# A third pair of split-weight tiles in two weight rings, a smaller scratch for dynamic DMAs, and new ranks and paces for interleaved streams

## The chip, the core and the metric

The kernel is one program on one core of a Trainium2 chip. TensorE (PE in the profile) multiplies matrices, with its weight loads shown apart as PEld; VectorE (DVE) and ScalarE (ACT) work on elements, GpSimd (POOL) fills tiles and issues the DMAs of its own queue, and SyncE (SP) issues the loads. Each engine runs its own instructions in program order, and waits where an operand or a tile is not free yet. The metric is device time in microseconds (us) of one execution; lower is better.

## What is computed

Two layers of a hybrid transformer trunk over 512 latent tokens and 256 context tokens, model width 1024, all in float32. The reference, cut to one layer:

```
mod  = silu(c) @ w_mod[l] + b_mod[l]                 # six vectors of 1024; the same for the context
h    = modulate(rmsnorm(x,   norm1_g[l]), sh1, sc1)  # 512 latent tokens
hc   = modulate(rmsnorm(ctx, norm1_g[l]), ...)       # 256 context tokens
y, yc = hybrid_mixer(h, hc, ...)   # one input projection, then side by side:
#   (A) gated DeltaNet, 8 heads, both directions: short conv, chunks of 64 with a triangular solve
#       in each, then a scan over the chunks; the latent scan starts from the context's last state
#   (B) latent attention, 8 heads: latent queries attend to context and latent keys
#   then one output projection of both
x = x + g1 * y
x = x + g2 * swiglu(modulate(rmsnorm(x, norm2_g[l]), sh2, sc2), w_gate[l], w_up[l], w_down[l])
# the context goes through the same output projection and FFN, in layer 0 only
return rmsnorm(x, final_norm_g)                      # after both layers
```

## The kernel before

**Split weights.** The large products run as three products of float32r tiles: a weight tile `w` is split into `hi` (a copy in float32r) and `lo = w - hi`, and so are the activations; `gemm` (L195) issues `hi*hi`, `hi*lo` and `lo*hi` for each block of 128 rows. `load_w` (L174) loads a weight in pieces of 512 columns: a DMA on SP into a raw tile (L183), a copy on ACT for `hi` (`cpy`, which the profile shows as L132), and a subtraction on DVE for `lo` (`tt`, shown as L120). There are two rings of these tiles: ring `w` for the latent stream (raw `wr`, halves `wh` and `wl`) and ring `f` for the context stream (`fr`, `fh`, `fl`). A ring holds two pairs `hi`/`lo`; `RAWS` (L45) gives ring `w` two raw tiles and ring `f` three. A weight of 1024 columns takes two pieces, so it fills a ring. A third way to load, ring `g`, brings a weight unsplit and is used only by the context's first input projection.

`pipelined` (L209) emits the load of weight i+1, its copies and subtractions too, just before the matmuls of weight i. A new tile of a ring waits until the last reader of the tile whose place it takes is done.

**Streams.** The program's order is made by `weave` (L59). Each part of the network is a generator, a stream, that emits some instructions and then yields either a condition to wait for or a triple: how long the piece lasts, what it costs TensorE, and what it costs VectorE, in the planner's own microseconds. `weave` keeps a time for each stream and one clock for each of the two engines, and takes next the stream with the smallest

```
    s = min(ready, key=lambda r: (max(r.t, clock[0]), r.rank, r.t))
    ...
    end = s.t + r[0]
    for i, c in enumerate(r[1:]):
        clock[i] = max(clock[i], s.t) + c
        end = max(end, clock[i])
```

so that among streams behind the TensorE clock the rank decides, the lower one first, and each piece pulls its stream up to both clocks. The streams that matter here, with their ranks before: `ctx_chain` and `lat_chain` (0; `gdn_pre`, with the triangular solve in 31 steps on DVE and transposes around it, then `gdn_scan`), `ctx_in`, `ctx_mla` and `mod_rest` (1; the modulation vectors, 16 units of 1 MB of weights each after the first 8), `lat_in` (2; normalize, then 20 input projections of one 1024-column weight each), `ctx_ffn` and `ctx_in1` (3), `mla_prep` (4; queries, keys and row maxima of four head pairs), `mla_att` (5; attention of the four pairs), `lat_ffn` (6). `mod_rest`, `lat_in`, `lat_chain`, `ctx_chain`, `mla_prep`, `mla_att` and `lat_ffn` exist once for each layer. `paced` (L1293) multiplies the triples of a stream by a factor: 0.6 for `lat_chain` and 1.5 for `mla_prep`, in layer 1 only.

In the order of time: context input projections; latent input projections with the context chain and `mod_rest` between them; `ctx_mla`; `ctx_ffn` with the first latent chain; attention of layer 0; `lat_ffn` with `ctx_in1` and the second context chain; layer 1 with `lat_in`, the latent chain and attention; at last `lat_ffn` alone.

**DMAs of POOL.** GpSimd issues the DMAs that copy rotary parts between tiles (`fill_rope`, L798), spill activations (L236, L1077) and bring the gates' rows back broadcast over partitions (L450). For the descriptors of these dynamic DMAs, a scratch is set aside in each partition of the on-chip memory.

Of the kernel before, what the change touches and what calls it, by code (L numbers as in the profile page):

```python
# [41 lines left out]
LAT = SimpleNamespace(n=NL, nch=8, off=NC_, mi=0, h="hx", t="t", w="w")  # L42
BUFS = {"hx": 16, "m": 12, "g4": 16, "hd": 7, "t": 4, "ox": 7, "kc": 4, "tc": 3, "st": 1}
WIDTH = {"hx": 512, "m": 512, "g4": 1024, "hd": 512, "t": 516, "ox": 512, "kc": 256, "tc": 260, "st": 512}
RAWS = {"w": 2, "f": 3}  # L45
PSB = {"A": 2, "M": 1, "F": 1, "B": 2, "C": 2}
CHUNK_AT = {("tail", 0): 0, ("ckv", 0): 17, ("cq", 0): 18, ("cq", 1): 19}
CHUNK_AT.update({(m, j): 1 + 4 * j + i for j in range(4) for i, m in enumerate("kqvz")})


PACE = {("lat_chain", 1): 0.6, ("mla_prep", 1): 1.5}


class Stream:
# [32 lines left out]
def trunk_kernel(ctx, tc, xin, cc, wmod, small, win, wuq, wuk, wuv, wout, wgu, wdn, cst, rope, out):  # L87
# [16 lines left out]
    def nm(s):  # L104
        uid[0] += 1
        return f"{s}_{uid[0]}"
# [67 lines left out]
    def load_w(src, n, ring):  # L174
        if ring == "g":
            big = slot("g4")
            nc.sync.dma_start(out=big[:, 0:n], in_=src)
            return big
        halves = []
        for a in range(0, n, 512):  # L180
            m = min(512, n - a)
            raw = raw_tile(ring)[:, 0:m]
            nc.sync.dma_start(out=raw, in_=src[:, a:a + m])  # L183
            hi = wp.tile([P, 512], F32R, name=nm(ring + "h"), tag=ring + "h", bufs=2)[:, 0:m]
            lo = wp.tile([P, 512], F32R, name=nm(ring + "l"), tag=ring + "l", bufs=2)[:, 0:m]
            cpy(hi, raw)
            tt(lo, raw, hi, SUB)
            halves.append((hi, lo))
        return halves
# [940 lines left out]
    def ctx_in():  # L1130
        v.xc = load_x(CTX, xin[:, :, 0:NC_])
        v.mod = [Mod(0)]
        for _ in v.mod[0].ticks(8, "g4"):
            pass
        v.xx = load_x(LAT, xin[:, :, NC_:])
        yield 35, 0, 21.0
        hc = modulated(CTX, v.xc, v.mod[0].al[:, 0], v.mod[0].t, 0, "F", True)
        v.c = [Mix(0, CTX, hc, [CALL], True, "A", "hd", "hd")]
        yield 5, 0, 3.0
        yield from v.c[0].inproj([("tail", 0)] + KQV[CALL], "g")  # L1140
        done.add("ckqv")
        yield from v.c[0].inproj(CQS + ZS, "g")
        done.add("cin")

    def ctx_chain(l):
        yield need("ckqv" if l == 0 else "c1kv")
        c = v.c[l]
        yield from c.stage(CALL)
        yield from c.scan(CALL)
        done.add(f"cscan{l}")  # L1150
        if l == 0:
            yield need("cin")
            c.gate(CALL)
            done.add("cg")

    def ctx_mla():
        yield need("cin")
        c = v.c[0]
        v.kvc = [mla_norm(0, CTX, [c.ckv], 8.0, KN, "F")[0]]
        cqc = mla_norm(0, CTX, c.cq, 4.0, QN, "F")  # L1160
        v.K = [keys(CTX, c.kr)]
        yield 6, 0, 3.6
        v.yc = []
        yield need("mod0")
        yield from mla_ctx(0, cqc, v.kvc[0], *v.K[0], v.yc)
        done.add("cmla")

    def ctx_ffn():
        yield need("cg", "cmla", "norm0")
        c, modt = v.c[0], v.mod[0].t  # L1170
        ys = ysplit(CTX, [c.o[j] for j in range(4)] + v.yc)
        v.xc = load_x(CTX, xin[:, :, 0:NC_])
        yield 5, 0, 3.0
        yield from outproj(0, CTX, ys, v.xc, modt, "FM")
        h2 = modulated(CTX, v.xc, v.mod[0].al[:, 1], modt, 24, "F")
        yield 8, 0, 4.8
        yield from ffn(0, CTX, v.xc, h2, modt, ("F", "M"))
        v.cs = dp.tile([KD, P, NC_], F32, name=nm("cscr"), tag=nm("cscr"))
        spill(v.xc, v.cs)
        done.add("cffn")  # L1180

    def ctx_in1():
        yield need("cffn", "att30")
        nmod = Mod(1)
        v.mod.append(nmod)
        yield from nmod.ticks(8, "m")
        done.add("head1")
        yield need("out0")
        v.xc = load_x(CTX, v.cs)
        hc = modulated(CTX, v.xc, nmod.al[:, 0], nmod.t, 0, "F")  # L1190
        c = Mix(1, CTX, hc, [CALL], False, "F", None, None)
        v.c.append(c)
        yield 8, 0, 4.8
        yield from c.inproj([("tail", 0)] + [(m, hj) for hj in range(4) for m in "kv"])
        done.add("c1kv")
        yield from c.inproj([("ckv", 0)])
        v.kvc.append(mla_norm(1, CTX, [c.ckv], 8.0, KN, "F")[0])
        v.K.append(keys(CTX, c.kr))
        done.add("c1")

    def mod_rest(l):
        yield need("cin" if l == 0 else "start1")
        yield from v.mod[l].ticks(16, "m")
        done.add(f"mod{l}")
# [85 lines left out]
            yield need("c1", "cscan1")  # L1290
            done.add("start1")

    def paced(gen, l):  # L1293
        f = PACE.get((gen.__name__, l), 1)
        for r in gen(l):
            yield r if callable(r) else tuple(f * a for a in r)

    streams = [(1, ctx_in()), (1, ctx_mla()), (3, ctx_ffn()), (3, ctx_in1())]
    for l in range(DEPTH):
        streams += [(0, ctx_chain(l)), (1, mod_rest(l)), (2, lat_in(l)), (0, paced(lat_chain, l)),  # L1300
                    (4, paced(mla_prep, l)), (5, mla_att(l)), (6, lat_ffn(l))]
    weave(streams)
    xx = v.xx
    pr = rms_rows(LAT, xx, 1.0, "A")
    for k in range(KD):
# [123 lines left out]
```

## Time and profile before

| | |
|---|---|
| median of 3 runs | 2268.44 us (2268.09 to 2271.84) |
| the profiled execution | 2272.16 us, of which 2270.4 us from the first to the last instruction |
| TensorE busy | 2090.8 us (92% of the span) |
| VectorE busy | 1448.1 us (64%) |
| ScalarE busy | 885.3 us (39%) |
| granted TensorE clock, mean | 0.953 of full speed |

Busy time is the time in which the profile shows an instruction of the engine at work. A busy TensorE is not TensorE at its peak: at a lower granted clock the same matmul is busy for longer.

### The profile page before, as it was taken

The numbers are of one execution on the slowest core, as the hardware profiler recorded it, in microseconds if no ns is written. First come the engines' busy times: TensorE is split into PE (matmuls) and PEld (weight loads), VectorE is DVE, ScalarE is ACT, GpSimd is POOL, SyncE is SP. The second block draws the span as 40 slices with busy tenths as digits, with TensorE's granted clock in tenths as the row PEclk, the third lists the DMA queues.
The fourth block names the chain that finished last, engine by engine and source line by source line (L and its number), as shares of the span: only waits on it lengthen the run. The fifth ranks groups of instructions, "written<-read, shape, count | busy, mean of one in ns | idle before, by whom it ended". The sixth has DMA issues, their size and how long they took to land.

```text
span 2270.4 us, 40544 instructions
## 1 busy us (share of the span) xinstructions
PE 2090.8 (92%) x16016; PEld 1616.3 (71%) x16016; DVE 1448.1 (64%) x2846; ACT 885.3 (39%) x1579; POOL 134.3 (6%) x307
## 2 busy tenths in 40 slices
PE   6989988899999999899999999996987998999996
PEld 3856677789887646678788885675654676888885
DVE  4668758976787653788544447898667355444445
ACT  3342355443435344552332234435343234222233
POOL 0200003000201000010000000200020000000000
PEclk9999998899999999999999999997997999999998
DMA  8336513343433143252222336531010012333322
GB/s 328 116 112 202 185 29 109 116 141 113 139 121 109 48 131 110 74 159 89 85 79 89 98 94 231 166 104 41 20 47 13 30 65 70 98 98 97 95 96 88
DMA packets 130639, 240.43 MB, mean 106 GB/s; under 512 B 15184, under 2 KB 30064, under 8 KB 130448
## 3 DMA queue, kind: packets, MB, share of 16 engines
q1 hardware_dynamic: 124592, 224.10, 30.4%
q0 software_dynamic: 5856, 13.74, 2.3%
q8 instruction: 126, 2.06, 0.4%
q14 instruction: 65, 0.53, 0.1%
HBM read 228.24 MB, written 6.91 MB: 104 GB/s over the span
## 4 chain that ended last, share of the span: by engine, by line
PE 74%; DVE 14%; DMA 5%; ACT 4%; issue 3%; SPq 0%; ACTq 0%; DVEq 0%; POOL 0%; POOLq 0%
PE psA L202 31%; PE psM L202 14%; PE psF L202 5%; PE psA L952 4%; PE psA L207 3%; PE psB L949 3%; PE psM L271 2%; PE psB L598 2%; DVE g L120 2%; DVE wl L120 1%; PE psC L645 1%; ACT t L132 1%; DVE g L129 1%; PE psC L668 1%; DVE fl L120 1%
## 5 line engine op out<-in xcount | busy, mean ns | idle before, releaser
L202 PE MATMUL psA<-hx,wh 128*128 128x512 f32 x1680 | 546.5, 403 | 26.8 <-ACT hx L132 17.0
L132 ACT ACTIVATE wh<-wr 128x512 fp32r<-128x512 f32 (+2 forms) x410 | 249.1, 608 | 674.6 <-PE psA L202 439.1
L120 DVE TENSOR_TENSOR wl<-wr,wh 128x512 fp32r<-128x512 f32 (+2 forms) x410 | 272.2, 665 | 244.2 <-ACT wh L132 241.8
L202 PEld LDWEIGHTS psA<-hx,wh 128*128 128x128 f32 x1680 | 316.7, 191 | 124.7 <-issue 20.7
L202 PE MATMUL psA<-hx,wl 128*128 128x512 f32 x840 | 333.9, 398 | 7.0 <-DVE wl L120 7.0
L202 PE MATMUL psM<-hx,wh 128*128 128x512 f32 x704 | 217.9, 390 | 1.5 <-ACT wh L132 1.5
L202 PEld LDWEIGHTS psA<-hx,wl 128*128 128x128 f32 x840 | 160.4, 191 | 49.4 <-DVE wl L120 10.4
L132 ACT ACTIVATE fh<-fr 128x512 fp32r<-128x512 f32 (+3 forms) x186 | 111.1, 600 | 170.5 <-PE psF L202 72.8
L129 DVE SCALAR_TENSOR_TENSOR g<-psA,mod,g 128x512 f32<-128x512 f32 x112 | 84.0, 750 | 111.4 <-PE psA L202 111.1
L120 DVE TENSOR_TENSOR fl<-fr,fh 128x512 fp32r<-128x512 f32 (+3 forms) x186 | 122.5, 660 | 48.2 <-ACT fh L132 42.6
L202 PEld LDWEIGHTS psM<-hx,wh 128*128 128x128 f32 x704 | 131.9, 188 | 29.7 <-ACT wh L132 2.8
L202 PE MATMUL psM<-hx,wl 128*128 128x512 f32 x352 | 137.4, 390 | 1.1 <-DVE wl L120 1.1
L202 PE MATMUL psF<-m,fh 128*128 128x256 f32 x600 | 115.1, 288 | 10.2 <-ACT m L132 7.4
L202 PE MATMUL psA<-hd,wh 128*128 128x512 f32 x384 | 120.6, 393 | 0.0
L952 PE MATMUL psA<-t,m 128*128 128x512 f32 x192 | 107.8, 670 | 3.9 <-ACT t L132 3.7
L202 PEld LDWEIGHTS psF<-m,fh 128*128 128x128 f32 x600 | 94.4, 192 | 17.6 <-ACT m L132 8.7
L202 PE MATMUL psA<-ox,wh 128*128 128x512 f32 x320 | 100.7, 393 | 0.0
L132 ACT ACTIVATE t<-psB 128x512 f32<-128x512 f32 x96 | 56.3, 596 | 91.4 <-PE psB L949 79.2
L202 PE MATMUL psF<-m,fl 128*128 128x256 f32 x300 | 86.8, 289 | 0.9 <-DVE fl L120 0.7
L202 PE MATMUL psM<-m,fh 128*128 128x256 f32 x416 | 83.7, 299 | 3.9 <-ACT m L132 2.1
L202 PEld LDWEIGHTS psA<-hd,wh 128*128 128x128 f32 x384 | 71.6, 188 | 16.7 <-DVE hd L120 1.1
L207 PE MATMUL psA<-m,g 128*128 128x256 f32 x320 | 74.4, 393 | 6.2 <-DMA g<-win 4.0
(378 smaller groups left out, 3710.8 us busy)
## 6 DMA issues: line engine op xcount, KB each, us to landing
wr<-wgu SPq DMA_DIRECT2D x176, 256.0 KB, 2.6
m<-wmod SPq DMA_DIRECT2D x160, 256.0 KB, 4.2
fr<-wgu SPq DMA_DIRECT2D x88, 256.0 KB, 2.7
wr<-win SPq DMA_DIRECT2D x80, 256.0 KB, 3.1
wr<-wdn SPq DMA_DIRECT2D x64, 256.0 KB, 2.6
g<-win SPq DMA_DIRECT2D x20, 512.0 KB, 6.6
g<-wmod SPq DMA_DIRECT2D x16, 512.0 KB, 10.2
fr<-wdn SPq DMA_DIRECT2D x32, 256.0 KB, 2.8
```

The source lines that it names most:

```text
L120: (e or V).tensor_tensor(out=out, in0=a, in1=b, op=op)
L129: V.scalar_tensor_tensor(out=out, in0=a, scalar=s, in1=b, op0=op0, op1=op1)
L132: A.activation(out, a, f, **kw)
L202: PE.matmul(o, ww[:, wk], xx if n is None else xx[:, a:a + n], start=cnt == 0, stop=cnt == 3 * nk - 1)
L207: PE.matmul(o, w[:, k * P:k * P + P], x_, start=k == 0, stop=k == len(xs) - 1)
L271: PE.matmul(o[32 * j:32 * j + 32, :], sc[:, k, :], parts[j], start=k == 0, stop=k == KD - 1, tile_position=(0, 32 * j))
L598: PE.matmul(pv[s, q, d, :], u3(lh[d])[s, c, :], u3(rh[d])[s, c, :], start=True, stop=True)
L645: PE.matmul(o[s], x_[s], y_[s], start=i == 0, stop=i == len(mm) - 1)
L668: PE.matmul(v4(kv)[s, hi, d, :], u3(ks[d])[s, unit(hi, n, d), :], v4(u)[s, hi, d, :], start=True, stop=True)
L949: PE.matmul(pst, K[ki][:, b:b + P], Q[qi], start=cnt == 0, stop=cnt == 2)
L952: PE.matmul(py, v.vt[i, j][:, hp:hp + 2, :].rearrange("p z e -> p (z e)"), pt, start=i == 0, stop=i == 5)
```

## The change

Both rings get a third pair of `hi`/`lo` tiles, and ring `w` a third raw tile. These are 10 KB more in each partition (five tiles of 512 float32). The scratch for dynamic DMAs is given a size, 2048 bytes. The table `TUNE` takes the place of the ranks in the code and of `PACE`: it names a rank and a pace for each stream and layer. Against before these entries differ: `ctx_mla` has rank 0 (was 1); `ctx_ffn` pace 0.93 (was 1); `lat_in` pace 2.0 in both layers (was 1); `mla_prep` pace 1.07 in layer 0 (was 1), and in layer 1 rank 2 (was 4) and pace 1.275 (was 1.5); `mod_rest` of layer 1 pace 0.7 (was 1). Everything else of the planner is as before.

```diff
-RAWS = {"w": 2, "f": 3}
+RAWS = {"w": 3, "f": 3}
...
-PACE = {("lat_chain", 1): 0.6, ("mla_prep", 1): 1.5}
+TUNE = {
+    ("ctx_in", 0): (1, 1.0),
+    ("ctx_mla", 0): (0, 1.0),
+    ("ctx_ffn", 0): (3, 0.93),
+    ("ctx_in1", 0): (3, 1.0),
+    ("ctx_chain", 0): (0, 1.0),
+    ("mod_rest", 0): (1, 1.0),
+    ("lat_in", 0): (2, 2.0),
+    ("lat_chain", 0): (0, 1.0),
+    ("mla_prep", 0): (4, 1.07),
+    ("mla_att", 0): (5, 1.0),
+    ("lat_ffn", 0): (6, 1.0),
+    ("ctx_chain", 1): (0, 1.0),
+    ("mod_rest", 1): (1, 0.7),
+    ("lat_in", 1): (2, 2.0),
+    ("lat_chain", 1): (0, 0.6),
+    ("mla_prep", 1): (2, 1.275),
+    ("mla_att", 1): (5, 1.0),
+    ("lat_ffn", 1): (6, 1.0),
+}
...
-            hi = wp.tile([P, 512], F32R, name=nm(ring + "h"), tag=ring + "h", bufs=2)[:, 0:m]
-            lo = wp.tile([P, 512], F32R, name=nm(ring + "l"), tag=ring + "l", bufs=2)[:, 0:m]
+            hi = wp.tile([P, 512], F32R, name=nm(ring + "h"), tag=ring + "h", bufs=3)[:, 0:m]
+            lo = wp.tile([P, 512], F32R, name=nm(ring + "l"), tag=ring + "l", bufs=3)[:, 0:m]
...
-    streams = [(1, ctx_in()), (1, ctx_mla()), (3, ctx_ffn()), (3, ctx_in1())]
-    for l in range(DEPTH):
-        streams += [(0, ctx_chain(l)), (1, mod_rest(l)), (2, lat_in(l)), (0, paced(lat_chain, l)),
-                    (4, paced(mla_prep, l)), (5, mla_att(l)), (6, lat_ffn(l))]
-    weave(streams)
+    once = (ctx_in, ctx_mla, ctx_ffn, ctx_in1)
+    per_layer = (ctx_chain, mod_rest, lat_in, lat_chain, mla_prep, mla_att, lat_ffn)
+    todo = [(g, 0, ()) for g in once] + [(g, l, (l,)) for l in range(DEPTH) for g in per_layer]
+    weave([(TUNE[g.__name__, l][0], paced(g(*a), TUNE[g.__name__, l][1])) for g, l, a in todo])
...
-    nc = bacc.Bacc("TRN2", target_bir_lowering=False, num_devices=1)
+    nc = bacc.Bacc("TRN2", target_bir_lowering=False, num_devices=1, dynamic_dma_scratch_size=2048)
```

## Rows read from the trace of the kernel before

**Rows 1.** The page: busy time, granted clock in 40 slices, chain that ended last.

```profile
PE 2090.8 (92%) x16016; PEld 1616.3 (71%) x16016; DVE 1448.1 (64%) x2846; ACT 885.3 (39%) x1579; POOL 134.3 (6%) x307
...
PEclk9999998899999999999999999997997999999998
...
PE 74%; DVE 14%; DMA 5%; ACT 4%; issue 3%; SPq 0%; ACTq 0%; DVEq 0%; POOL 0%; POOLq 0%
```

**Rows 2.** Windows by stage: length, busy us and instructions by engine, granted clock, DMA.

```profile
113.00:340.00 227.00, 210.00 (x1860) 148.35 (x1860) 167.42 (x352) 99.94 (x191) 14.61 (x54) 0.97 0.41 132
340.00:398.00 58.00, 48.74 (x555) 41.75 (x550) 50.62 (x108) 31.11 (x63) 18.80 (x26) 0.85 0.36 110
398.00:740.00 342.00, 314.31 (x3664) 288.21 (x3664) 265.90 (x579) 153.68 (x282) 24.57 (x43) 0.94 0.40 124
...
965.00:1135.00 170.00, 162.38 (x1294) 133.42 (x1292) 126.23 (x266) 67.75 (x124) 10.11 (x24) 0.99 0.36 111
1135.00:1365.00 230.00, 230.00 (x1306) 188.53 (x1305) 104.82 (x158) 68.94 (x115) 0.00 (x0) 1.00 0.29 90
1365.00:1532.00 167.00, 160.39 (x965) 112.71 (x964) 138.76 (x264) 70.31 (x118) 25.64 (x64) 0.97 0.53 169
1532.00:1830.00 298.00, 249.57 (x2861) 166.83 (x2859) 195.42 (x413) 112.54 (x199) 21.70 (x36) 0.87 0.10 29
...
1932.00:2230.00 298.00, 298.00 (x1312) 245.48 (x1311) 136.19 (x205) 89.48 (x147) 0.00 (x0) 1.00 0.31 96
```

**Rows 3.** Timeline of the last FFN, one ring turn: start, us, instruction, idle before.

```profile
2003.99 0.63 ACT L132 ACTIVATE wh<-wr 128x512 fp32r<-128x512 f32 x1 [2.07 <-PE psA L202]
...
2004.88 0.68 DVE L120 TENSOR_TENSOR wl<-wr,wh 128x512 fp32r<-128x512 f32 x1
```

**Rows 4.** TensorE's waits over the whole run: total us, times, longest.

```profile
PE psA L202 <- DVE wl L120: 7.0, 7, 3.8
...
PE psM L202 <- DVE fl L120: 3.7, 6, 1.2
...
PE psF L202 <- DVE fl L120: 2.5, 2, 1.8
...
PE psA L767 <- DVE wl L120: 2.3, 1, 2.3
...
PE psM L202 <- ACT fh L132: 1.5, 2, 0.9
...
PE psM L202 <- ACT wh L132: 1.5, 3, 1.0
...
PE psA L202 <- ACT wh L132: 1.2, 1, 1.2
...
PE psM L202 <- DVE wl L120: 1.1, 2, 0.9
```

**Rows 5.** Timeline of the context FFN, one ring turn that stalls TensorE.

```profile
641.30 0.63 ACT L132 ACTIVATE fh<-fr 128x512 fp32r<-128x512 f32 x1 [0.81 <-PE psF L202]
...
642.03 0.68 DVE L120 TENSOR_TENSOR fl<-fr,fh 128x512 fp32r<-128x512 f32 x1
...
642.77 0.39 PE L202 MATMUL psM<-hd,fl 128*128 128x256 f32 x1 [1.16 <-DVE fl L120]
```

**Rows 6.** Timeline of layer 1's input projections, the longest ring wait.

```profile
1463.08 0.63 ACT L132 ACTIVATE wh<-wr 128x512 fp32r<-128x512 f32 x1
...
1469.92 0.68 DVE L120 TENSOR_TENSOR wl<-wr,wh 128x512 fp32r<-128x512 f32 x1
...
1470.66 0.79 PE L202 MATMUL psA<-hx,wl 128*128 128x512 f32 x1 [3.78 <-DVE wl L120]
```

**Rows 7.** Timeline of layer 1, end of a triangular solve.

```profile
1544.61 2.04 DVE L555 STREAM_TRANSPOSE g<-g 128x1024 f32<-128x1024 f32 x1
...
1546.75 0.23 PE L563 MATMUL psB<-g,g 32*32 32x32 f32 x1 [6.04 <-issue]
```

**Rows 8.** TensorE's waits, the scans: total us, times, longest.

```profile
PE psC L668 <- DVE g L120: 7.6, 4, 4.1
```

**Rows 9.** DMA issues: count, KB each, median us to landing.

```profile
g<-gscr POOLq DMA_DIRECT2D x24, 256.0 KB, 4.7
...
hx<-hx POOLq DMA_DIRECT2D x16, 64.0 KB, 1.9
```

More of the change, by code (lines that the diff above doesn't have):

```diff
@@ L1291, in lat_ffn, with paced @@
             done.add("start1")
-    def paced(gen, l):
-        f = PACE.get((gen.__name__, l), 1)
-        for r in gen(l):
+    def paced(gen, f):
+        for r in gen:
             yield r if callable(r) else tuple(f * a for a in r)
-    streams = [(1, ctx_in()), (1, ctx_mla()), (3, ctx_ffn()), (3, ctx_in1())]
-    for l in range(DEPTH):
-        streams += [(0, ctx_chain(l)), (1, mod_rest(l)), (2, lat_in(l)), (0, paced(lat_chain, l)),
-                    (4, paced(mla_prep, l)), (5, mla_att(l)), (6, lat_ffn(l))]
-    weave(streams)
+    once = (ctx_in, ctx_mla, ctx_ffn, ctx_in1)
+    per_layer = (ctx_chain, mod_rest, lat_in, lat_chain, mla_prep, mla_att, lat_ffn)
+    todo = [(g, 0, ()) for g in once] + [(g, l, (l,)) for l in range(DEPTH) for g in per_layer]
+    weave([(TUNE[g.__name__, l][0], paced(g(*a), TUNE[g.__name__, l][1])) for g, l, a in todo])
     xx = v.xx
```

## The prediction

> **What bounds the kernel now.** I read the page first. TensorE is busy 92% of the span and three quarters of the chain that ended last is its own work [rows 1], so time comes only from what TensorE loses: stretches in which it stands idle, and stretches in which it runs at a lower granted clock. The clock has two levels, 2.4 GHz and 1.2 GHz; a mean of 0.87 says that in some 26% of that stretch it was the lower one, and half of that time was lost if TensorE was busy. As a formula, a stretch of length W with mean clock c loses (1 - c)W.
>
> The windows by stage say where. The two long FFN stretches (1135 to 1365 and 1932 to 2230) show 230.00 of 230 and 298.00 of 298 us busy at clock 1.00 [rows 2]: nothing can be gained there, and these 528 us are a floor. 298 us over 1312 matmuls is 227 ns for one of 512 columns, so a 1024-column weight (24 matmuls) takes 5.45 us and a piece of 512 takes 2.7 us; for the context's 256 columns I estimate half, 1.36 us a piece. The other six stages of rows 2, 1262 us together, lose 17.0 + 9.3 + 27.7 + 7.6 + 6.6 + 48.4 = 116.6 us of idle time (length less busy) and, by the formula, 6.8 + 8.7 + 20.5 + 1.7 + 5.0 + 38.7 = 81.4 us of clock. That is the pool, 198 us, and for each microsecond of idle time 0.70 us of clock were lost beside it. I price a stall that goes at 1.70 times its length; that the clock follows the idle time so evenly is an assumption.
>
> **The third pair.** It removes no work and adds none; it lets the copy of a piece start one piece earlier. In the FFN, one turn reads: ACT's copy sat idle 2.07 us until TensorE released the tile, then 0.63 us of copy and 0.68 us of subtraction [rows 3]. That wait lies on ACT, and the 1.31 us hide behind 2.7 us of matmuls of the other pair: worth nothing there. In the context FFN the same 1.31 us, plus the hand-overs between engines, stands against only 1.36 us of matmuls, so any other work on ACT or DVE at that moment stalls TensorE: copy at 641.30, subtraction at 642.03, and a matmul that waited 1.16 us [rows 5]. Here a third pair gives 1.36 us of slack. Cost of this cause over the whole run: the waits of TensorE for wl, fl, wh and fh are 7.0 + 3.7 + 2.5 + 2.3 + 1.5 + 1.5 + 1.2 + 1.1 = 20.8 us [rows 4]. This is the upper bound of what goes directly. The lower bound is zero, since the order of instructions on DVE stays, and some subtractions are late because DVE is behind, not because the tile is late: in rows 6 the copy was done at 1463.7 and the subtraction began at 1469.9, 6 us later, and a third pair moves neither. Taking off that wait (3.8 us) leaves 17; I take 13, nearer the upper end because rows 5 show the pattern that the pair mends and they are the more frequent kind. With the clock: 13 x 1.70 = 22 us.
>
> A repeated gap in one stage and none in another is how the Trainium skill (Perfetto Trace Analysis, Optimization Strategy) recognizes too few buffers. The trace has that gap in the context FFN and not in the latent one. By the rule alone all 20.8 us would go, 35 us with the clock, and the sum below would be 49 instead of 36.
>
> The third raw tile lets SP issue one load earlier in ring w. No wait for a wr load is among the rows that cost TensorE anything, so I take 0.
>
> **The smaller scratch.** It touches only POOL's DMAs, which land in 1.9 us (rotary parts) to 4.7 us (gate rows) [rows 9]. Cost 0, if their descriptors still fit; the other case is a rival below.
>
> **The order.** lat_in at pace 2 charges 10.24 us on TensorE's clock for a projection instead of 5.12. That does not give the chain beside it twice the pieces. Each piece pulls its stream up to the clocks: after a projection the chain is behind, emits a piece and stands at the clock, emits one more and stands 1 us beyond it, and the projection is next. Worked through by hand, I get two solve steps for each projection, as before. What the pace does change is the start of lat_in: its normalizing piece charges DVE 12 us instead of 6, and until the first projection mod_rest gets about two more of its units. In layer 0, mod_rest then ends about two projections earlier, ctx_mla (rank 0 now) starts as much earlier beside lat_in, and some 11 us of projections (2 x 5.45) are left to lie beside the ctx_mla tail at 340 to 398, which idles 9.3 us at clock 0.85 [rows 2]. Bounds: 0, and 9.3 + 8.7 = 18 us. I take 4, since both have work for DVE, which is busy 50.6 of the 58 us there. In layer 1 two earlier units cover little idle time (6.6 us in all); 0.
>
> The rank of mla_prep in layer 1 (2 for 4) decides nothing: lat_in, the only stream between, is done when mla_prep begins. Its pace does: a piece charged 7.5 is charged 6.4, so the number of solve steps between two of its pieces falls by about 15%, and TensorE has other work nearer when a solve ends. Such an end cost 6.04 us of idle TensorE, with the transposes of DVE running until 1546.65 before the matmul at 1546.75 [rows 7]. Bounds: a gain of all that the stage from 1532 to 1830 loses, 48.4 + 38.7 = 87 us, and a loss of 33 us (rival 2). I take that one stall: 6.04 x 1.70 = 10 us. ctx_ffn at 0.93 and mla_prep of layer 0 at 1.07 shift pieces by less than one; 0.
>
> **Sum:** 22 + 4 + 10 = 36 us. The profiled execution took 2272.2 us, so 2236; the median of the runs shown is 3.7 us lower, so 2232.
>
> **Rivals.**
> 1. Nothing to measure. The ring's waits return under another name, since DVE's order stays [rows 6], and the moves cancel. Gain about 3 us: 2265. For it: only 20.8 us of waits carry the ring's name. Against it: rows 5.
> 2. Slower: the end of layer 1. With mla_prep earlier, attention runs ahead of the chain, and the last scan of eight chunks stands alone. A scan step without cover cost up to 4.1 us of idle TensorE [rows 8]; 8 x 4.1 = 33 us. With the ring's 22 us and without the other two terms: 2272 + 33 - 22 = 2283 profiled, 2279 as a median. It decides from the point at which fewer than eight attention pieces are left when that scan begins. For it: the stage at 1532 to 1830 has the most loss already. Against it: 15% of the distance between pieces is little.
> 3. Much faster: the new order mends half of what layer 1 loses at 1532 to 1830, 43 us instead of 10: 2203 profiled, 2199 as a median. For it: the size of that pool. Against it: no single row shows what would do it.
> 4. The scratch is too small and POOL's DMAs queue for room. Eight attention pairs wait once for a rotary copy (8 x 1.9) and six chain groups for their gate rows (6 x 4.7): 43 us. 2236 + 43 = 2279 profiled, 2275 as a median. The Trainium skill (DMA: Bandwidth & Descriptors, SWDGE vs HWDGE vs iDMA) says that the rings of software-made descriptors live in such a carveout of the on-chip memory. Nothing in this trace shows the rings filling.
>
> **How the numbers follow.** My forecast 0.53, rivals 0.13, 0.14, 0.15 and 0.05 in that order. The forecast's own range is 2210 to 2255: the ring from 0 to its bound of 35 us and the order terms from about 0 to 24. For 8 in 10 it reaches into rivals 2 and 3: 2192 to 2280. A difference of 0.2% (4.5 us) is about what can be told from no change here. Faster: 0.53 + 0.15 + a third of rival 1 (0.04) = 0.72; the rest of rival 1 is the same, 0.09; slower 0.14 + 0.05 = 0.19.
>
> **What would show it.** In the changed profile, TensorE's waits for fl and fh nearly gone and idle time at the context FFN down by about 8 us; waits for wl like that of rows 6 still there; the two FFN stretches unchanged in length; POOL's landings still at 1.9 and 4.7 us; the wait before L563 in layer 1 shorter. The prediction is wrong if the ring's waits go and the span stays, if the scans of layer 1 stand alone at its end, or if the stage after 1532 gains several times the 10 us that I give it.

## The result and the profile after

The changed kernel takes 2256.73 us as a median of 7 runs (2249.52 to 2262.01), beside 2268.44 us (2266.59 to 2274.47) for the kernel before. The ratio is 0.994, with a 95% interval of 0.9927 to 0.9952: 13.6 us less (0.006 x 2268.44), where 36 us were forecast. The profiled execution took 2256.73 us, its span 2255.0 us. Lines below the new table stand 19 further down: the matmuls of `gemm` are L221 for L202, ACT's copy is L151 for L132, DVE's subtraction L139 for L120, the solve's first matmul L582 for L563.

The page of the changed kernel: busy time, clock in 40 slices, chain that ended last.

```profile
PE 2070.9 (92%) x16016; PEld 1606.8 (71%) x16016; DVE 1451.2 (64%) x2846; ACT 888.7 (39%) x1583; POOL 132.9 (6%) x307
...
PEclk9999998999999999999999999998898998999998
...
PE 72%; DVE 13%; DMA 5%; ACT 5%; issue 3%; SPq 0%; POOL 0%; ACTq 0%; DVEq 0%; POOLq 0%
```

The same matmuls take 2070.9 us instead of 2090.8 [rows 1]. TensorE's idle time, span less busy, is 184.1 us; it was 179.6. So the time did not come out of the idle time in sum.

The windows of the changed kernel, with the cuts of [rows 2] and the stretch from 1830 to 1932, which those rows leave out: length, busy us by engine, granted clock, DMA.

```profile
113.00:340.00 227.00, 211.55 (x1842) 151.31 (x1841) 169.12 (x356) 102.01 (x197) 16.93 (x59) 0.98 0.42 134
340.00:398.00 58.00, 50.19 (x559) 44.50 (x557) 50.00 (x101) 33.40 (x65) 15.47 (x21) 0.88 0.42 121
398.00:740.00 342.00, 303.64 (x3324) 274.78 (x3323) 271.30 (x591) 149.03 (x273) 24.89 (x43) 0.95 0.37 117
965.00:1135.00 170.00, 165.82 (x1316) 137.47 (x1315) 128.16 (x271) 68.84 (x127) 10.29 (x25) 0.99 0.36 112
1135.00:1365.00 230.00, 230.00 (x1306) 188.55 (x1305) 109.00 (x166) 70.83 (x120) 1.66 (x3) 1.00 0.29 92
1365.00:1532.00 167.00, 157.23 (x960) 110.85 (x959) 136.26 (x261) 67.71 (x114) 23.05 (x61) 0.99 0.51 163
1532.00:1830.00 298.00, 251.44 (x2893) 171.08 (x2892) 200.33 (x418) 117.97 (x206) 21.77 (x36) 0.89 0.11 32
1830.00:1932.00 102.00, 92.95 (x391) 74.60 (x390) 52.75 (x79) 38.69 (x60) 0.00 (x0) 0.93 0.26 84
1932.00:2230.00 298.00, 298.00 (x1312) 245.33 (x1311) 138.60 (x211) 92.33 (x154) 0.00 (x0) 1.00 0.30 94
```

The two floors stand, 230.00 and 298.00 us at clock 1.00. The window with the context FFN, 398 to 740, is worse: 38.4 us idle instead of 27.7. The cuts are fixed in time and the work shifts under them, so stages are compared further down by what begins and ends them.

TensorE's waits for the rings in the changed kernel (total us, times, longest), all of them; those of before are [rows 4].

```profile
PE psA L221 <- DVE wl L139: 8.9, 6, 3.1
...
PE psM L221 <- DVE fl L139: 3.7, 4, 1.4
...
PE psF L221 <- DVE fl L139: 1.7, 4, 0.9
...
PE psF L221 <- ACT fh L151: 0.2, 1, 0.2
...
PE psM L221 <- DVE wl L139: 0.2, 1, 0.2
```

They sum to 14.7 us, 6.1 us less than the 20.8 of [rows 4]. The waits for copies (`wh`, `fh`) went from 4.2 us to 0.2; those for subtractions (`wl`, `fl`) only from 16.6 to 14.5.

The timeline of the changed kernel at the end of the triangular solve of [rows 7].

```profile
1541.37 1.91 DVE L574 STREAM_TRANSPOSE g<-g 128x1024 f32<-128x1024 f32 x1
...
1543.53 0.23 PE L582 MATMUL psB<-g,g 32*32 32x32 f32 x1 [7.44 <-DVE g L574]
```

The stall that was to go is there, 7.44 us instead of 6.04.

The DMA issues of POOL in the changed kernel: count, KB each, median us to landing.

```profile
g<-gscr POOLq DMA_DIRECT2D x24, 256.0 KB, 5.5
...
hx<-hx POOLq DMA_DIRECT2D x16, 64.0 KB, 2.3
```

Against [rows 9] that is 0.8 and 0.4 us more. The smaller scratch is not the reason: ring_only (below), which has it, shows 4.6 and 1.9, and order_only, which has not, 5.2 and 2.0. None of the DMAs that TensorE waits for is one of these: they are loads of weights (`win`, `wmod`).

### The profile page after: what moved, and what is told of

Read it like the earlier page. It is cut to its first block, busy times and chain, and to the rows that moved or that the text cites. A ratio compares the mean times of both kernels' runs of the same rounds, so it can differ in the third digit from the quotient of the medians.

```text
span 2255.0 us, 40566 instructions
## 1 busy us (share of the span) xinstructions
PE 2070.9 (92%) x16016; PEld 1606.8 (71%) x16016; DVE 1451.2 (64%) x2846; ACT 888.7 (39%) x1583; POOL 132.9 (6%) x307
## 4 chain that ended last, share of the span: by engine, by line
PE 72%; DVE 13%; DMA 5%; ACT 5%; issue 3%; SPq 0%; POOL 0%; ACTq 0%; DVEq 0%; POOLq 0%
PE psA L221 33%; PE psM L221 14%; PE psA L971 4%; PE psF L221 4%; PE psB L968 3%; PE psA L226 2%; PE psM L290 2%; DVE g L148 2%; PE psB L617 2%; ACT t L151 2%; PE psC L664 1%; DVE fl L139 1%; ACT L151 1%; DVE g L139 1%; PE psC L676 1%
## 5 line engine op out<-in xcount | busy, mean ns | idle before, releaser
L221 PE MATMUL psA<-hx,wh 128*128 128x512 f32 x1680 | 541.0, 400 | 19.8 <-ACT hx L151 16.1
L151 ACT ACTIVATE wh<-wr 128x512 fp32r<-128x512 f32 (+2 forms) x410 | 248.9, 608 | 636.0 <-PE psA L221 452.7
L139 DVE TENSOR_TENSOR wl<-wr,wh 128x512 fp32r<-128x512 f32 (+2 forms) x410 | 270.3, 660 | 228.4 <-ACT wh L151 227.9
L221 PEld LDWEIGHTS psA<-hx,wh 128*128 128x128 f32 x1680 | 313.8, 190 | 115.7 <-ACT hx L151 18.6
L221 PE MATMUL psA<-hx,wl 128*128 128x512 f32 x840 | 332.3, 396 | 8.9 <-DVE wl L139 8.9
L221 PE MATMUL psM<-hx,wh 128*128 128x512 f32 x704 | 219.8, 391 | 0.0
L221 PEld LDWEIGHTS psA<-hx,wl 128*128 128x128 f32 x840 | 159.3, 190 | 50.1 <-DVE wl L139 12.0
L151 ACT ACTIVATE fh<-fr 128x512 fp32r<-128x512 f32 (+3 forms) x186 | 110.7, 600 | 152.8 <-PE psF L221 41.6
L221 PEld LDWEIGHTS psM<-hx,wh 128*128 128x128 f32 x704 | 132.8, 189 | 27.2
L139 DVE TENSOR_TENSOR fl<-fr,fh 128x512 fp32r<-128x512 f32 (+3 forms) x186 | 121.3, 657 | 45.5 <-ACT fh L151 42.6
L221 PE MATMUL psM<-hx,wl 128*128 128x512 f32 x352 | 137.9, 392 | 0.2 <-DVE wl L139 0.2
L221 PE MATMUL psF<-m,fh 128*128 128x256 f32 x600 | 118.7, 292 | 14.1 <-ACT m L151 9.9
L221 PE MATMUL psA<-hd,wh 128*128 128x512 f32 x384 | 120.5, 393 | 0.0
L221 PEld LDWEIGHTS psF<-m,fh 128*128 128x128 f32 x600 | 96.4, 194 | 22.5 <-ACT m L151 12.5
L221 PE MATMUL psA<-ox,wh 128*128 128x512 f32 x320 | 100.7, 393 | 0.0
L151 ACT ACTIVATE t<-psB 128x512 f32<-128x512 f32 x96 | 56.5, 595 | 96.9 <-PE psB L968 84.4
L221 PE MATMUL psF<-m,fl 128*128 128x256 f32 x300 | 86.4, 288 | 1.3 <-DVE fl L139 1.3
L221 PE MATMUL psM<-m,fh 128*128 128x256 f32 x416 | 77.9, 285 | 9.1 <-ACT m L151 8.1
L221 PEld LDWEIGHTS psA<-hd,wh 128*128 128x128 f32 x384 | 71.7, 188 | 16.4 <-DVE hd L139 1.0
## 6 DMA issues: line engine op xcount, KB each, us to landing
g<-wmod SPq DMA_DIRECT2D x16, 512.0 KB, 10.2
```

The source lines that it names most:

```text
L139: (e or V).tensor_tensor(out=out, in0=a, in1=b, op=op)
L151: A.activation(out, a, f, **kw)
L221: PE.matmul(o, ww[:, wk], xx if n is None else xx[:, a:a + n], start=cnt == 0, stop=cnt == 3 * nk - 1)
```

## The experiments

Eighteen kernels were run, each with some 5 to 12 executions beside the kernel before on the same chip; all of them compute the whole reference. "Rings" stands for the third pairs, the third raw tile and the scratch together. "us" is (ratio less 1) times the median of the kernel before that ran beside it, so minus is faster; an interval of the ratio is about 3 us to either side. The kernels ran on several chips, ring_only on one, so a comparison of two of them rests on these ratios.

| kernel | median us | ratio (95%) | us |
|---|---|---|---|
| the change | 2256.73 | 0.994 (0.9927 to 0.9952) | -13.6 |
| ring_only | 2255.07 | 0.9914 (0.9902 to 0.9927) | -19.6 |
| order_only | 2281.54 | 1.0027 (1.001 to 1.0044) | +6.1 |
| pairs_only | 2261.19 | 0.9952 (0.9939 to 0.9964) | -10.9 |
| raw_only | 2267.89 | 0.9976 (0.9965 to 0.9986) | -5.5 |
| ring_w | 2265.39 | 0.9964 (0.9948 to 0.9979) | -8.2 |
| ring_f | 2269.93 | 0.9984 (0.9972 to 0.9996) | -3.6 |
| order_l0 | 2261.62 | 0.9943 (0.993 to 0.9955) | -13.0 |
| order_l1 | 2254.11 | 0.9904 (0.9889 to 0.9919) | -21.8 |
| l1_prep | 2251.24 | 0.991 (0.9897 to 0.9923) | -20.4 |
| l0_latin | 2263.61 | 0.9964 (0.9951 to 0.9978) | -8.2 |
| no_latin0 | 2264.58 | 0.9974 (0.996 to 0.9988) | -5.9 |
| l0_lat11 | 2269.65 | 0.9991 (0.998 to 1.0002) | -2.0 |
| lat11_old | 2283.52 | 1.0042 (1.0027 to 1.0056) | +9.6 |
| l0_lat15 | 2268.54 | 0.9974 (0.9962 to 0.9986) | -5.9 |
| l0_mla | 2263.0 | 0.9955 (0.9939 to 0.9972) | -10.2 |
| l0_ffnprep | 2263.88 | 0.9961 (0.9946 to 0.9976) | -8.9 |
| chain_early | 2260.58 | 0.9938 (0.9924 to 0.9952) | -14.1 |
| rings_chain09 | 2263.36 | 0.9954 (0.9941 to 0.9968) | -10.5 |

**The two halves of the change.** ring_only is the kernel before with the rings; order_only is the changed kernel without them.

```diff
 ring_only, against before
-RAWS = {"w": 2, "f": 3}
+RAWS = {"w": 3, "f": 3}
-... tag=ring + "h", bufs=2)
+... tag=ring + "h", bufs=3)
-... tag=ring + "l", bufs=2)
+... tag=ring + "l", bufs=3)
-... num_devices=1)
+... num_devices=1, dynamic_dma_scratch_size=2048)
 order_only, against the change: the same lines the other way
```

> The kernel before with the third pairs, the third raw tile and the smaller scratch; ranks and paces as before. Ring theory (the third pair carries the gain, and the order adds little): 9 to 13 us faster than before, about 2257 us, with TensorE's waits for wl, wh, fl and fh at 14 us or less in total instead of 20.8. Order theory (the new ranks and paces carry it): within 4 us of before, about 2267 us. Canceling theory (the pair was worth its 22 us and the new order spent half of it again): about 2246 us, faster than the full change.

> The full change with two pairs in each ring, two raw tiles in ring w and the scratch of before; the new ranks and paces. Ring theory: within 4 us of before, about 2267 us. Order theory: about 2257 us, as the full change. Canceling theory: slower than before by some 10 us, about 2279 us.

The rings give 19.6 us and the order costs 6.1. The sum, -13.5, is what the whole change measured (-13.6). The rings are worth as much under the new order (6.1 + 13.6 = 19.7 us) as under the old. So the order term has the wrong sign, and the rings alone are faster than the change.

TensorE's waits for the rings in ring_only, all of them.

```profile
PE psA L202 <- DVE wl L120: 8.0, 4, 4.0
...
PE psF L202 <- DVE fl L120: 3.1, 4, 1.1
...
PE psM L202 <- ACT fh L132: 1.1, 1, 1.1
...
PE psA L202 <- ACT wh L132: 0.8, 1, 0.8
...
PE psM L202 <- DVE fl L120: 0.5, 2, 0.2
...
PE psF L202 <- ACT fh L132: 0.4, 1, 0.4
...
PE psM L202 <- DVE wl L120: 0.2, 1, 0.2
```

These are 14.1 us, 6.7 less than in [rows 4]. A gain of 19.6 us came with 6.7 us of waits by the rings' name. The page of ring_only, the line to set beside that of [rows 1]:

```profile
PE 2074.9 (92%) x16016; PEld 1608.4 (71%) x16016; DVE 1445.6 (64%) x2846; ACT 886.2 (39%) x1581; POOL 133.5 (6%) x307
```

Its span is 17.1 us shorter (2253.3 for 2270.4), and of these only 1.2 are idle time of TensorE: 15.9 are busy time of the same 16016 matmuls.

**Which ring, which tile.** pairs_only leaves ring `w` at two raw tiles, raw_only leaves the pairs at two, ring_w and ring_f give a third pair to one ring (ring_w with the raw tile). All have the scratch and the order of before.

```diff
 pairs_only, against ring_only
-RAWS = {"w": 3, "f": 3}
+RAWS = {"w": 2, "f": 3}
 raw_only, against before (and the scratch)
-RAWS = {"w": 2, "f": 3}
+RAWS = {"w": 3, "f": 3}
 ring_w, against ring_only (both halves; ring_f: "f" for "w", and RAWS as before)
-bufs=3
+bufs=3 if ring == "w" else 2
```

> The kernel before with the smaller scratch and the third pair in both rings, but two raw tiles in ring w. With the raw tile, the pairs gave 19.6 us; the raw tile alone gave 5.5 us. If the two add up: 12 to 16 us faster than before. If the pairs need the raw tile to be filled in time: 8 us or less. By the forecast (raw tile worth 0): 19 us or more.

> The kernel before with the smaller scratch and the third raw tile of ring w; two pairs in both rings. By the forecast the raw tile is worth 0: within 4 us of before. If early loads are what counts: 10 us faster or more.

> The kernel before with the smaller scratch, a third raw tile and a third pair in ring w (latent weights) only; ring f keeps two pairs, ranks and paces as before. Both rings together gave 19.6 us. If the gain lies in the context FFN, as the forecast's first term has it: 3 to 7 us faster than before, the rest being ring f's. If it lies in the latent stages (in the trace with both rings layer 0 up to 940 us gained 5 us, the rest came later): 12 to 17 us faster than before.

> The kernel before with the smaller scratch and a third pair in ring f (context weights) only; ring w keeps two pairs and two raw tiles. If the gain lies in the context FFN: 13 to 17 us faster than before. If it lies in the latent stages: 3 to 7 us faster.

The pairs give 10.9 us and the raw tile, priced at 0, gives 5.5 (each with the small scratch, whose share was not measured by itself); 16.4 together, within the intervals of 19.6. Ring `f`, the context's, to which the working gave most of the 22 us, gives 3.6 alone; ring `w` with its raw tile 8.2. These two do not add: they make 11.8 singly and 19.6 together, so that ring `f`'s pair is worth 3.6 us alone and 11.4 beside ring `w`'s. In the context FFN itself (first to last down projection) the pair does what the working said, on a smaller scale. TensorE's waits for `fl` and `fh` there are 7.0 to 7.9 us with two pairs (before, raw_only, ring_w) and 3.3 to 4.1 with three (ring_f, pairs_only, ring_only, order_l1, l1_prep), and this stage takes 252.4 to 255.8 us with two and 246.4 to 252.5 with three, 4.5 us less in the mean.

One place of ring `w`'s gain repeats in every kernel. From the last attention piece of layer 1 to the last FFN it takes 69.1 to 69.6 us in the four kernels without a third pair in ring `w` and with the old layer-1 order (before, raw_only, ring_f, lat11_old), and 61.4 to 61.5 in the ten others with that order. The window of that stretch before, then in ring_only (columns as in [rows 2]).

```profile
1821.70:1891.20 69.50, 54.43 (x223) 41.85 (x221) 39.90 (x64) 27.67 (x43) 0.00 (x0) 0.88 0.18 61
```

```profile
1809.60:1871.10 61.50, 49.41 (x212) 38.21 (x210) 34.58 (x56) 24.95 (x39) 0.00 (x0) 0.91 0.21 69
```

The waits of TensorE in it, before and in ring_only (the other large one, 10.6 us for `hx`, is in both).

```profile
PE psC L700 <- DVE ro1y L129: 3.1, 1, 3.1
```

```profile
PE psC L700 <- DVE ro1y L129: 0.7, 1, 0.7
```

3.0 us of idle time and 3 us of clock go here, and the wait that shrinks is named for a tile of the chain's output (`ro1y`), not for a weight. The last FFN, to its last up projection, then takes 344.7 us for 341.4, so 4.7 of the 8 stay. The forecast's pool left most of this stretch out, as it left out 1830 to 1932. No one place holds the 17.1 us between the two profiles: ring_only is 5.2 us ahead where the latent FFN begins, gains 3.5 more up to layer 1's attention, 3.4 in it and 8.0 in this stretch, and gives 3.0 back in what follows.

What changed the neighbours of a weight's instructions? The order in which DVE's instructions stand in the built program, ring_only against before, from its first lines:

```
## DVE: 2786 rows in the other, 2791 in this; 2858 lines of difference
...
 L120 TENSOR_TENSOR wl_1005<-wr_1002,wh_1004 128x512
 L129 SCALAR_TENSOR_TENSOR m_262<-m_262 128x64
+L120 TENSOR_TENSOR wl_1011<-wr_1008,wh_1010 128x512
+L124 TENSOR_SCALAR m_262<-m_262 128x64 x2
 L120 TENSOR_TENSOR fl_2252<-fr_2249,fh_2251 128x256
-L124 TENSOR_SCALAR m_262<-m_262 128x64 x2
+L362 RECIPROCAL m_262<-m_262 128x64
```

`weave` is the same in both kernels and emits the same instructions in the same order, and yet a subtraction for the next weight stands ahead of a chain's operations where it stood later. On the way from `weave`'s order to the engines' queues instructions are moved once more, and the number of tiles in a ring enters into it. On TensorE the listing has 1517 lines, 1037 for ring_w, 562 for ring_f and 256 for raw_only. It prints the lines around a difference too: some 860 of the 1517, and some 1570 of DVE's 2858, are rows that moved, each counted where it left and where it came. With the scratch alone (built, not run) both engines' orders are those of before.

**The two halves of the order.** order_l0 is the change with layer 1's entries as before, order_l1 with layer 0's entries as before, l1_prep the rings with only `mla_prep` of layer 1 at (2, 1.275).

```diff
 order_l0, against the change
-("mod_rest", 1): (1, 0.7), ("lat_in", 1): (2, 2.0), ("mla_prep", 1): (2, 1.275)
+("mod_rest", 1): (1, 1.0), ("lat_in", 1): (2, 1.0), ("mla_prep", 1): (4, 1.5)
 order_l1, against the change
-("ctx_mla", 0): (0, 1.0), ("ctx_ffn", 0): (3, 0.93), ("lat_in", 0): (2, 2.0), ("mla_prep", 0): (4, 1.07)
+("ctx_mla", 0): (1, 1.0), ("ctx_ffn", 0): (3, 1.0), ("lat_in", 0): (2, 1.0), ("mla_prep", 0): (4, 1.0)
 l1_prep, against order_l1
-("mod_rest", 1): (1, 0.7), ("lat_in", 1): (2, 2.0)
+("mod_rest", 1): (1, 1.0), ("lat_in", 1): (2, 1.0)
```

> The full change with the entries of layer 1 (mod_rest, lat_in, mla_prep) as before, so that only the entries of layer 0 are new. If the 10 us that appear between 1530 and 1830 us in the trace of the full change come from the entries of layer 1, as the forecast's third term has it: about 2267 us. If they come from the third pair: about 2257 us, as the full change.

> The full change with the entries of layer 0 (ctx_mla, ctx_ffn, lat_in, mla_prep) as before, so that only the entries of layer 1 are new. In the trace of the full change layer 0 up to 930 us gained about 1 us, with two new stalls of 7.7 and 6.4 us of TensorE at 419 and 615 us. If the entries of layer 0 made these stalls and the third pair alone had gained there: faster than the full change by 10 us or more, about 2245 us. If the third pair itself brought them: about 2257 us.

> Third pairs, raw tile and scratch; of the new entries only mla_prep of layer 1 (rank 2, pace 1.275). By the forecast's third term: 10 us faster than the third pairs alone, ratio 0.987, with the stall before the matmul that follows the first solve of layer 1 (4.8 us with the third pairs alone) gone. If the pace only moves the stall: ratio 0.990 to 0.992, the same as the third pairs alone.

Layer 1's entries give 2 us over the rings alone (-21.8 against -19.6), and `mla_prep`'s pace, priced at 10, gives 1: neither can be told from nothing. Layer 0's cost 6.6. In l1_prep the attention stage of layer 1 does shorten, from 211.1 to 203.5 us, and the stretch behind it grows from 61.5 to 66.9: work was moved over the boundary. order_l1, the rings with layer 0 as before, has the lowest ratio, but it can't be told from l1_prep and ring_only; all three are faster than both kernels.

**Layer 0, entry by entry.** Each of these has the rings and the order of before but for the entry named; no_latin0 is the change with `lat_in` of layer 0 back at 1.0, lat11_old is l0_lat11 without the rings.

```diff
 against the rings alone
 l0_latin    ("lat_in", 0): (2, 2.0)
 l0_lat11    ("lat_in", 0): (2, 1.1)
 l0_lat15    ("lat_in", 0): (2, 1.5)
 l0_mla      ("ctx_mla", 0): (0, 1.0)
 l0_ffnprep  ("ctx_ffn", 0): (3, 0.93), ("mla_prep", 0): (4, 1.07)
```

> Both third pairs, raw tile and smaller scratch; of the new entries only lat_in of layer 0 at pace 2.0, all others as before. All entries of layer 0 together cost 6.6 us against the third pairs alone (ratio to before 0.9914). If lat_in's pace is what costs: ratio 0.993 to 0.995. If it is the gain of some 4 us that the forecast's second term has, and ctx_ffn, mla_prep or ctx_mla cost more than it gives: ratio 0.989 to 0.990.

> The full change with only lat_in of layer 0 put back to pace 1.0. On top of the third pairs (ratio to before 0.9914) lat_in at 2.0 alone cost 11 us, all layer 0 entries together 6.6 us, and the layer 1 entries gave 2 us. If these add up: ratio 0.988 to 0.990, about 2247 us, faster than every kernel so far. If entries do not add up because each new order is drawn afresh: anywhere between 0.990 and 0.996.

> Third pairs, raw tile and scratch; of the new entries only lat_in of layer 0, at pace 1.1 instead of 2.0. If the price of 11 us is that of a larger charge for each projection, a tenth of the step costs little: ratio 0.991 to 0.993, near the third pairs alone (0.9914). If any change of the order in layer 0 draws a new one, with no regard to its size: as far from 0.9914 as with pace 2.0, on either side.

> The kernel before with one entry of the order: lat_in of layer 0 at pace 1.1; two pairs, two raw tiles in ring w, no given scratch. It is l0_lat11 without the rings' part. Theory (the rings' gain is the same under any order): slower than the kernel before by the 17.5 us that this entry cost with the new rings, 2288 us, ratio 1.008. Rival (the gain depends on which order the rings meet): the 17.5 us are a clash of this entry with the third pairs, and without them the entry costs little, 2270 us, ratio 1.000 (0.998 to 1.003).

> The new rings, the order of before, and lat_in of layer 0 at pace 1.5. Known beside the rings alone: pace 1.1 costs 17.5 us, pace 2.0 costs 11. Theory (each pace gives another order of instructions, whose cost has no relation to the pace): anywhere from 0 to 20 us more than the rings alone, ratio 0.991 to 1.000, with other stalls than either. Rival (a longer planned projection costs by itself, in steps): between its neighbours, 11 to 17.5 us more, ratio 0.996 to 0.999.

> The new rings, the order of before, and only the rank of ctx_mla, 0 for 1. The four entries of layer 0 together cost 7 us, lat_in's alone 11. Theory (entries don't add): a cost or a gain of its own of up to 10 us either way, and the sum of the single entries misses 7. Rival (entries add): this one and the pair ctx_ffn and mla_prep together give back 4 us, so each is within 5 us of the rings alone, ratio 0.989 to 0.9935, and their sum is a gain.

> The new rings, the order of before, and only ctx_ffn at 0.93 and mla_prep of layer 0 at 1.07. The prediction gave both nothing. Theory (entries don't add, each is another order): a cost or a gain of up to 10 us, ratio 0.987 to 0.996. Rival (entries add): together with the rank of ctx_mla a gain of 4 us, ratio about 0.990 with that of ctx_mla about 0.991.

Against ring_only these cost 11.4 (pace 2.0), 13.7 (1.5), 17.6 (1.1), 9.4 (the rank of `ctx_mla`) and 10.7 us (the pair). They don't add: pace 2.0, the rank and the pair make 31.5 us singly and 6.6 together (order_l0), and taking `lat_in`'s pace out of the change makes that 7.7 us slower. Nor do they grow with the change: a pace of 1.1 costs more than one of 2.0. lat11_old lies between its two expectations: the entry costs 9.6 us without the rings, and they give 11.6 us under this order, not 19.6.

**Where layer 0 loses.** How far a single profile can be read shows in kernels that have the same instructions in the same order up to layer 1: the latent FFN begins at 941.0, 945.8 and 939.7 us in ring_only, order_l1 and l1_prep, and at 940.9 and 946.7 in the change and order_l0. So some 6 us there mean nothing, and the 6.6 us that layer 0's entries cost in the medians can't be found by comparing the change with ring_only at that point. Yet in the traces up to here one place parts the kernels. In all eight with layer 0's order as before, the second triangular solve of the latent chain ends 9 to 13 us before the last down projection of the context FFN, and from there to the latent FFN it takes 228.4 to 231.0 us. In all ten with another order (the change among them) the solve ends 5 to 35 us after it, and it takes 233.6 to 244.3. The windows that begin at the context FFN's end, 40 us, in the change and then in ring_only.

```profile
700.90:740.90 40.00, 32.50 (x245) 19.30 (x248) 33.98 (x75) 15.25 (x30) 5.29 (x10) 0.83 0.09 27
```

```profile
701.00:741.00 40.00, 37.65 (x686) 28.84 (x685) 25.57 (x47) 17.90 (x35) 7.20 (x14) 0.97 0.29 90
```

7.5 us idle at clock 0.83 against 2.4 at 0.97: 14.3 us are lost against 3.6. Two kernels tested whether this place is the cost. chain_early brings the solve back under the context FFN in the new order; rings_chain09 changes much of the old order (a listing of 3079 lines on TensorE) and leaves the solve covered.

```diff
 chain_early, against the change
-    ("lat_chain", 0): (0, 1.0),
+    ("lat_chain", 0): (0, 0.7),
 rings_chain09, against the rings alone
-    ("lat_chain", 0): (0, 1.0),
+    ("lat_chain", 0): (0, 0.9),
```

> The full change with one more entry: lat_chain of layer 0 at pace 0.7 (was 1.0), so that the second latent chain is issued earlier. In TensorE's order of instructions its solve then ends with 58 matmuls of the context FFN still to come, as in the kernel before (66) and unlike in the full change (none). Theory (the new order costs because this solve ends after the context FFN is used up, with nothing beside it): the stretch from the context FFN's last down projection to the latent FFN falls from 237.7 to about 230 us, and the time by about as much: 2249 us, ratio 0.991 (0.989 to 0.9925). Rival (any other order than the one before costs 7 to 17 us, wherever it differs): no better than the full change, ratio 0.994 to 0.998, with the stretch at 234 us or more.

> The new rings, the order of before, and only lat_chain of layer 0 at pace 0.9. It changes 3079 lines of TensorE's order, about as much as the single entries of layer 0 that cost 9 to 17 us, but the second solve still ends with 66 matmuls of the context FFN to come. Theory (the uncovered solve is what costs): as fast as the rings alone within 4 us, ratio 0.9895 to 0.9932, the stretch from the context FFN to the latent FFN at 228 to 231 us. Rival (any other order costs): 7 to 17 us more, ratio 0.9945 to 0.999.

The solve ended 9.8 and 13.7 us before the context FFN's end, as meant, and the stretch behind it took 232.1 and 229.6 us. The times did not follow: 0.9938, no better than the change, and 0.9954, 9 us worse than the rings alone. The windows of the context FFN and of the stretch to the latent FFN: the change, chain_early, ring_only.

```profile
454.50:703.20 248.70, 229.10 (x2740) 216.17 (x2739) 185.16 (x395) 108.57 (x199) 21.35 (x37) 0.97 0.42 130
703.20:940.90 237.70, 216.36 (x1689) 135.56 (x1688) 134.62 (x253) 98.20 (x174) 7.43 (x15) 0.95 0.28 86
```

```profile
454.90:715.30 260.40, 238.03 (x2825) 221.83 (x2824) 207.70 (x450) 109.64 (x199) 21.67 (x37) 0.96 0.43 125
715.30:947.40 232.10, 213.95 (x1635) 135.93 (x1634) 119.54 (x214) 98.43 (x176) 7.04 (x15) 0.97 0.29 88
```

```profile
462.50:711.80 249.30, 230.03 (x2798) 216.92 (x2797) 195.39 (x423) 108.04 (x197) 21.32 (x37) 0.97 0.43 131
711.80:941.00 229.20, 212.88 (x1635) 135.22 (x1634) 118.33 (x213) 97.86 (x176) 7.05 (x14) 0.97 0.29 89
```

Against the change, the covered solve of chain_early took 5.6 us off the later stretch and put 11.7 on the context FFN, where now 85 more matmuls and 22.5 us more of DVE's work lie (207.70 for 185.16): the loss moved with the work. rings_chain09 has the solve covered and costs 9 us all the same. So the uncovered solve is a mark of the new orders and a place where they lose, not what decides their cost. That theory fell.

**One stall of the new order that has a name.** In nine of the ten kernels counted above with another order of layer 0 (not in l0_ffnprep) TensorE stands still once for 6.2 to 6.7 us in the context FFN; the eight with the old order show none over 4.2 us there. The timeline of it in the change.

```profile
611.73 2.69 POOL L139 TENSOR_TENSOR g<-g,g 128x1024 f32<-128x1024 f32 x1
...
613.00 2.52 DVE L902 CAST g<-kc 32x256 fp32r<-32x256 f32 x1
...
615.33 2.39 POOL L514 TENSOR_SCALAR_AFFINE_SELECT g<-g 64x1024 f32<-64x1024 f32 x2
615.53 1.13 DVE L145 TENSOR_SCALAR g<-t 32x256 fp32r<-32x256 f32 x1
616.67 1.19 DVE L902 CAST g<-kc 32x256 fp32r<-32x256 f32 x1
617.80 2.34 POOL L139 TENSOR_TENSOR g<-g,g 128x1024 f32<-128x1024 f32 x1
617.88 2.50 DVE L145 TENSOR_SCALAR g<-t 32x256 fp32r<-32x256 f32 x1
620.39 0.28 DVE L902 CAST g<-kc 32x256 fp32r<-32x256 f32 x1
620.60 0.41 DVE L139 TENSOR_TENSOR hd<-tc,hd 128x256 fp32r<-128x256 f32 x1
...
621.06 0.58 PE L221 MATMUL psM<-hd,fh 128*128 128x256 f32 x1 [6.41 <-DVE hd L139]
```

The new orders put the filling of attention's keys (`fill_keys`, L902 and the line behind it) beside GpSimd's preparation of the solve, and ahead of the `hd` that TensorE needs (in l0_latin and others it is an `fl`). Four small operations take 2.52 + 1.13 + 1.19 + 2.50 = 7.3 us; the one behind GpSimd's last takes 0.28. The same operation over the whole run, min/median/max ns, before and then in the change.

```profile
L883 DVE CAST g<-kc x8: 270/282/533, 589.3 to 1591.2; 32x256 fp32r<-32x256 f32 x8
```

```profile
L902 DVE CAST g<-kc x8: 274/283/2518, 613.0 to 1588.3; 32x256 fp32r<-32x256 f32 x8
```

At 0.28 us each these four cost 1.1 us, so 6.2 us are new, about the length of the stall. The stall also has the size of what the order costs without the rings (6.1), but that it is the cost is not shown, and more speaks against it: l0_ffnprep and rings_chain09 have no such stall (their longest in the context FFN are 3.9 and 4.3 us) and cost 10.7 and 9.1 us over the rings alone, and chain_early has none (3.3) and is no faster than the change.

## Why the prediction was right or wrong

**Right in sign, and little over a third of the size.** 13.6 us came of 36. The time, 2256.73 us, lies just above the forecast's own range (2210 to 2255) and inside the wide one (2192 to 2280), between the forecast and rival 1. The narrow range does not follow from its own bounds: with the ring and the order terms at 0 it would reach 2268.

**The step that failed** is the pricing of the order by hand: 14 us were forecast, 4 for layer 0 (`lat_in`'s pace, with `ctx_mla`'s rank) and 10 for `mla_prep`'s in layer 1. The order alone lost 6.1 us (order_only); by parts, layer 0's entries lost 6.6 and `mla_prep`'s gave 1. That is 20 of the 22 us that are missing; the rings' term missed by 2.4.

**The rings, forecast 22 us:** 19.6 under the old order and 19.7 under the new (11.6 under that of lat11_old), the right size in good part by luck. The working took 13 of 20.8 us of named waits, mostly in the context FFN, times 1.70. Measured: 6.1 to 6.7 us of named waits went, the context FFN itself became 4.5 us shorter, and idle time in sum hardly fell (179.6, ring_only 178.4). The Trainium skill's rule weighed there (Perfetto Trace Analysis, Optimization Strategy), by which a gap that keeps repeating can mean too few buffers, was priced at all 20.8; some two thirds of them stayed (14.1 in ring_only).

**The premise that failed under the rings' term** is "the order of instructions on DVE stays". It was the reason for the lower bound and for rival 1; some 1570 rows of DVE's order are taken out or put in by the rings alone. With a third pair a subtraction stands earlier among other work, and part of the gain lies in the neighbours: the stretch behind layer 1's attention gave 4.7 us net at a wait for `ro1y`, mostly in a part of the trace that the pool left out. That the changed placement is what turns 6.7 us into 19.6 fits all this but was not isolated, since no kernel here adds tiles without it.

**The third raw tile, forecast 0:** 5.5 us (0.9965 to 0.9986), with the scratch, which alone leaves the order as it was. The tile's load was on no wait of TensorE in [rows 4], and it moved rows of TensorE's order (the listing of 256 lines).

**The factor 1.70** for the clock is neither borne out nor refuted. The sum (1 - c) x span over the runs, 101.3 us as a mean for before, is 98.2 for ring_only and 94.7 for the change: the clock gave back some 3 to 7 us, where 0.70 of 13 us would be 9. In the two profiled executions alone it is 12.1 (106.7 before, 94.6 in ring_only). Single runs scatter by more than the differences, so the split is rough.

**The order in layer 0, forecast 4 us gained:** 6.6 us lost with the rings (order_l0). The hand-worked chain of reasons ended in a normalizing piece that costs 12 instead of 6. A kernel with that piece alone charged twice (built, not run) has TensorE's order unchanged, so the pace works through the projections, for which the working had "two solve steps for each projection, as before": l0_latin, with that pace alone, has another order on TensorE and costs 11.4 us. In the change the second solve ends at 738.0 instead of 704.7, and the context FFN, which starts 8.5 us earlier (454.5 for 463.0), is used up before it. `ctx_ffn` at 0.93 and `mla_prep` of layer 0 at 1.07, forecast 0, cost 10.7 us.

**`mla_prep` in layer 1, forecast 10 us:** 1 us, within the interval of none. The stall of [rows 7] stayed (7.44 us in the change; 5.34 in l1_prep for 4.76 in ring_only), and what the attention stage won the stage behind it lost.

**The rivals.** Rival 2 did not come: TensorE's waits at the scans fell (L687, 3.5 us in all and 1.2 at the longest, for the 7.6 and 4.1 of [rows 8]), and layer 1's entries cost nothing. Rival 3 did not come: the stage from 1532 lost 46.6 us idle instead of 48.4. Rival 4 did not come: every kernel with the rings has the small scratch, raw_only too, and they are faster, and POOL's DMAs land as fast with it (4.6 and 1.9 us in ring_only); the scratch alone was not run. Rival 1 named half of the truth, that the moves of the order bring nothing, for a wrong reason.

**What stays open.** Where the rest of the rings' gain comes from, some 10 us beside the 4.5 in the context FFN and the 4.7 behind layer 1's attention. Why each other order of layer 0 costs 9 to 18 us with the rings but all four entries 6.6, and why rings_chain09 is 9 us behind ring_only with all the marks of the good order. The stages show places (the uncovered solve, the key fill, the context FFN of chain_early), not one cause, and one profile of a stage can't settle differences of a few us. What the small scratch does by itself was not run.

## What to carry to other kernels

A buffer count is not only a buffer count: where something between the source and the engines orders instructions by when their tiles are free, one more tile reorders the work, so compare the built order of both kernels before pricing anything by "the order stays". Price a planner's knobs by runs, not by hand: here their effects neither added nor grew with the change, and a pace of 1.1 cost more than one of 2.0. When a change has a part that adds room and a part that retunes, run each alone; the room alone was faster here than the two together.

## What the runs showed of the hardware

The granted clock differs between runs of one and the same program, and the time with it: the twelve runs of order_only go from 2268.8 us at a mean clock of 0.961 to 2287.8 us at 0.952. A loss of (1 - c) x span is 88 us in the first and 110 in the second, 21 us apart for 19 us of time. So a change of 0.5% needs a median of several runs.

The same 32x256 cast on DVE took 0.28 us and 2.52 us, the long ones beside GpSimd's elementwise work. The Trainium skill (SBUF — State Buffer, Who interferes with whom) says that the two engines share a pair of ports, and that a DVE operation in a two-port mode, which casts can enter, and one of GpSimd hold it for a whole instruction while the other is blocked. The timeline above agrees with a lock: the 2.52 us lie beside GpSimd's work, and the first cast after it takes 0.28. In which mode the cast ran no row shows; GpSimd's spans in a profile are rough, and no run here took its work away to show the lock by itself.
